# A feed-forward block with Winograd products: seven product banks in four tiles, operands stored as two parts, sums kept per product

## The chip, the cores and the metric

The kernel runs on one core of a Trainium2 chip. The metric is the device time of one execution in microseconds (us). Engines: PE (TensorE: matmuls, with PEld for its weight loads), DVE (VectorE), ACT (ScalarE), POOL (GpSimd), SP (SyncE, which here issues most of the DMAs). Each works off its own queue of instructions in order. PSUM, into which PE writes, has 8 banks of 512 float32 on each of 128 partitions.

## The reference

One decoder layer in float32 for a prompt of 512 tokens and a group of 32 sample tokens: attention and a gated recurrence on one projection, cross attention, and a feed-forward block. The change touches the last:

```
hf = rmsnorm(x, p['norm_ffn_g'])
gate, up = jnp.split(hf @ p['w_gate_up'], 2, axis=-1)
x = x + (jax.nn.silu(gate) * up) @ p['w_down']
```

x has 544 tokens (512 + 32) of 2048 features; w_gate_up is 2048 x 11264, w_down 5632 x 2048.

## The kernel before

The feed-forward block takes the last half of the time. Tokens are the columns, in two halves of 272 (HT); features are on the partitions. Every float32 operand goes to PE as two exact parts, a rounded high one and the rest, and a product is three matmuls: high x high, high x low, low x high. On top of this stands one level of Winograd's scheme: two blocks of columns of the weights and a pair of feature blocks make a 2 x 2 of blocks, the two halves of the tokens the other 2 x 2, and seven products replace eight.

A **step** takes two pairs of feature blocks: 7 products x 2 pairs x 3 = 42 matmuls of 128x128 by 128x272. Gate/up has 44 blocks j of 128 hidden features, each of 4 steps; the down product has 22 pairs of hidden blocks in chunks of 4, 4, 4, 4 and 6 (`FFN_CHUNKS`), and in each chunk 8 pairs of columns m with 2 steps (3 in the last chunk). That makes 264 steps and 11,088 matmuls.

- `left` (L1603) makes a step's weights: two loads of 256 KB on SP into a tile u of eight 128x256 blocks (3 buffers; four of them raw, four for sums), four sums on GpSimd (L1613 to L1616), and for the raw ones and the sums apart a cast to the high part on ACT (`wh`, L1620, 128x768 and 128x1024) and a subtraction on DVE for the low part (`wl`, L1621). High and low parts have two buffers, so weights are made up to two steps ahead.
- `wino` (L1626) issues the matmuls (L1647). Its seven products lie in two tiles of two banks (`mm`, each with two buffers) and three single banks (`aux`). The products that need only raw weights come first, then the four with sums.
- `combine` (L1653) reads the banks: one copy on ACT (L1661) and seven adds of 272 columns on DVE; in the down product it adds to accumulators `acc`, with two more adds of 544 columns on GpSimd (L1670, L1671).
- `ffn` (L1682) runs over both products. After a block of gate/up come two multiplications, Silu on ACT (L1713) and a third (L1715), which makes the final u. After every odd block four sums of halves are made on GpSimd (L1572 to L1575, from L1616 on in the same queue as the weights' sums), and the pair goes to `hT` in DRAM by four DMAs on ACT's queue (L1719, L1721). In the down product `fetch` (L1688) brings a pair back by four loads on SP (L1696) and splits them into parts once more, on ACT (L1590) and DVE (L1591). It is called some steps ahead of the next chunk, as far as buffers are free (`PAIR_TAGS`, `DOWN_PLAN`).
- In the last chunk x is added (L1747) and `store_y` transposes the result on PE (L960), scales it on ACT (L1776) or DVE and stores it.

The order on each engine comes from a scheduler that works through the program by priorities; it is fixed when the kernel is built.

Of the kernel before, what the change touches and what calls it, by code (L numbers as in the profile page):

```python
# [8 lines left out]
F32 = mybir.dt.float32  # L9
# [24 lines left out]
PAIR_TAGS = [["ah"] * 7, ["ah"] * 5 + ["al"] * 2, ["al"] * 7, ["al"] * 3 + ["r"] * 4, ["ah"] * 4 + ["al"] * 3, ["al"] + ["h"] * 3 + ["t"] * 3, ["t"] * 7, ["t"] * 7]  # L34
# [36 lines left out]
def build_consts(c):  # L71
# [45 lines left out]
    # rows (head of two, 7 - batch, part, step) to columns (head of two, batch, step), both parts summed  # L117
# [4 lines left out]
    # rows (batch of four, part, head, step) to columns (head, batch of four, step): the head's own, both parts summed  # L122
# [17 lines left out]
def head_rows(c):  # L140
    """Per-head scalars: columns (chunk, head) on every partition, and two columns with rows (head, batch, step)."""
# [45 lines left out]
def weights(c, w, k0, nk, c0, n=P, kept=False, eng=None):  # L187
    """A block of weights, split exactly into two parts of 12 bits each: a pair for every feature block."""
# [13 lines left out]
def products(c, ps, w, k, act, first, last, n=P):  # L202
    """One block of a projection: w^T act, exact but for the product of the two low parts."""
# [11 lines left out]
def project(c, w, k0, c0, acts, n=P, step=8):  # L215
    """PSUM [n, 2, 272] = (rows k0.. of w, columns c0..c0+n)^T acts"""
# [14 lines left out]
def split(c, x, g, hi=None, lo=None):  # L231
    """x * g (g per partition) as two exact parts."""
# [13 lines left out]
class Stats:  # L246
    """Sum of squares over all features, for every token, on every partition."""
# [15 lines left out]
    def rstd(self, name, scale=None):  # L263
        """(mean + EPS) ** -0.5; with scale, what was added is scaled by it, and so is the root's reciprocal."""
# [81 lines left out]
def x_rstd(c, ss):  # L346
    """The reciprocal roots of the tokens' mean squares, from columns to rows on every partition."""
# [21 lines left out]
def first_projections(c):  # L369
    """Loads the tokens and projects them on the first head's q and k, feature block by feature block."""  # L370
# [20 lines left out]
class Side:  # L391
    """Work of the mixers, handed out in small steps between the blocks of the projections.

    A step yields (tensor engine time, time until its results are there), both estimates in us."""
# [59 lines left out]
    def finish(self, e, steps=1e9):  # L454
        """Runs one work to its end, or until so many of its steps are done."""
# [5 lines left out]
    def drain(self, some=None):  # L461
        """Runs all that is left, or until some is done."""
# [70 lines left out]
    # the sums of the keys behind, a block of keys after the other, each token's in its own column  # L533
# [21 lines left out]
def stick(c, z, n, sp=None):  # L555
    """softplus(z) and log(sigmoid(z)), each over n columns"""
# [18 lines left out]
def sb_sample(c, g):  # L575
    """Stick-breaking attention of the sample group, four heads: 512 paged keys and its own."""
# [12 lines left out]
    # own keys: rows (head, batch, step)  # L589
# [28 lines left out]
    # paged keys: columns (page, head, batch, step)  # L618
# [33 lines left out]
def parts(c, src, vector=True):  # L652
    """src [P, 512] as two exact parts."""
# [108 lines left out]
def load_pages(c, cache, pages, h0, nh):  # L762
    """[keys, (page, head, d)] of the given pages (indices into the table)."""
# [11 lines left out]
def gates(c, acts, rstd):  # L775
    """Decay and beta of the gated delta rule, with tokens on partitions."""
# [4 lines left out]
    # prompt: columns (a|b, chunk, head); sample: columns (a|b, stack), rows (head, batch, step)  # L781
# [28 lines left out]
    # running sums of log decay, totals, and their exponentials  # L810
# [22 lines left out]
    # per (head, batch) of the sample stacks, on every partition  # L833
# [7 lines left out]
def silu(c, x, out):  # L841
    """out = x * sigmoid(x), with exp and ln alone"""
# [135 lines left out]
def gdn_scalars(c, ssq, ssk, sel, n):  # L978
    """Per-token factors from the norms of q and k: columns of [P, n] tiles."""
# [17 lines left out]
def gdn_raw(c, m, ps, rstd):  # L997
    """One block of 128 channels before the short convolution, the prompt part after three zeros."""
# [12 lines left out]
def gdn_conv(c, m, raw):  # L1011
    """The short convolution of one block of 128 channels, prompt part."""
# [18 lines left out]
def gdn_head(c, h, qkv):  # L1031
# [20 lines left out]
    # decay between tokens, [j, chunk, i]  # L1052
# [74 lines left out]
def out_norm(c, f, so, n):  # L1127
    """f <- f * (mean((f * o)^2) + eps)^-0.5, with so = sum(o^2)"""
# [8 lines left out]
def gdn_sample(c, g):  # L1137
    """The gated delta rule for four heads of the sample group: rows (head, batch, step)."""
# [49 lines left out]
    # q and k on the states  # L1188
# [42 lines left out]
    # new states  # L1231
# [25 lines left out]
def conv_state(c):  # L1257
    """The last three rows before the convolution."""
# [36 lines left out]
def memory(c):  # L1295
    """Keys and values of the prompt's memory tokens."""
# [68 lines left out]
def softmax(c, ps, n, scale=None):  # L1365
    """ps [P, n, 256] -> normalized exp over the last axis, in SBUF [P, n * 256]; logits are SCALE * ps, or scale * ps (by row)."""
# [19 lines left out]
def cross_head(c, h, q, out, scale):  # L1386
    """Cross attention of the prompt group, one head; the result is scaled by token."""
# [38 lines left out]
def cross_sample(c, qs, outs, scale):  # L1426
    """Cross attention of the sample group: columns (batch, head, step); the result is scaled by token."""
# [54 lines left out]
def cross(c, acts, st, x, side):  # L1482
    """Cross attention and its output projection, in two parts of the tokens."""
# [5 lines left out]
    for h in range(4):  # L1489
# [6 lines left out]
        # from here on the tokens are scaled by these, so that their sums lose nothing  # L1496
# [49 lines left out]
def blocks(i):  # L1546
    """The two feature blocks of the i-th pair."""
# [399 lines left out]
```

## Time and profile before

| | |
|---|---|
| runs of before | 3057.8, 3061.66, 3063.03 us; median 3061.66 |
| the profiled execution's span | 3059.9 us |
| feed-forward block in it | from about 1511 us to the end |
| PE busy over the whole span | 95% |

"x" and a number behind a row is the count of instructions, then busy time and the mean duration of one in ns. In the windows each engine has its busy time and count, then the granted clock of PE as a share of full speed (PEclk), the busy share of the 16 DMA engines, and GB/s. In a timeline a row has its start and length in us; what stands in brackets is the engine's idle time just before it and what ended it. "ACTq" and "SPq" are the issues of DMAs on those queues.

### The profile page before, as it was taken

The numbers are of one execution on the slowest core, as the hardware profiler recorded it, in microseconds if no ns is written. First come the engines' busy times: TensorE is split into PE (matmuls) and PEld (weight loads), VectorE is DVE, ScalarE is ACT, GpSimd is POOL, SyncE is SP. The second block draws the span as 40 slices with busy tenths as digits, with TensorE's granted clock in tenths as the row PEclk, the third lists the DMA queues.
The fourth block names the chain that finished last, engine by engine and source line by source line (L and its number), as shares of the span: only waits on it lengthen the run. The fifth ranks groups of instructions, "written<-read, shape, count | busy, mean of one in ns | idle before, by whom it ended". The sixth has DMA issues, their size and how long they took to land.

```text
span 3059.9 us, 58347 instructions
## 1 busy us (share of the span) xinstructions
PE 2900.2 (95%) x22118; PEld 2789.1 (91%) x22118; DVE 2134.3 (70%) x3339; ACT 1363.5 (45%) x2600; POOL 1671.8 (55%) x1784
## 2 busy tenths in 40 slices
PE   8999999999999999999799999999999989988898
PEld 7999998889899999999689999999999989988797
DVE  6776775655655655366687777777777888888865
ACT  5544453435645654245543343333333344334333
POOL 3211122312112100032378988898888977999997
PEclk9999999999999999999899999999999999999999
DMA  7323233544535765423434344333434354344343
GB/s 212 95 80 85 75 88 99 144 137 147 173 105 151 227 197 150 127 81 116 161 117 127 118 122 123 121 117 118 125 118 123 116 179 132 110 131 127 119 137 105
DMA packets 619505, 392.67 MB, mean 128 GB/s; under 512 B 36475, under 2 KB 572360, under 8 KB 619224
## 3 DMA queue, kind: packets, MB, share of 16 engines
q1 hardware_dynamic: 596904, 355.95, 39.6%
q10 hardware_dynamic: 22320, 32.99, 3.0%
q8 instruction: 174, 2.85, 0.4%
q14 instruction: 107, 0.88, 0.1%
HBM read 334.17 MB, written 54.68 MB: 127 GB/s over the span
## 4 chain that ended last, share of the span: by engine, by line
POOL 27%; PE 20%; DVE 8%; issue 4%; DMA 4%; ACT 2%; SPq 0%; POOLq 0%; ACTq 0%; DVEq 0%
PE mm L208 7%; POOL u L1615 6%; POOL u L1613 6%; POOL u L1614 5%; PE mm L1647 5%; POOL u L1616 5%; PE aux L1647 4%; DVE wl L1621 3%; DMA u<-in_w_gate_up 2%; DVE pr L1591 2%; PE aux L1342 2%; POOL acc L1670 1%; PE mm L1530 1%; POOL x L1572 1%; PE aux L960 1%
## 5 line engine op out<-in xcount | busy, mean ns | idle before, releaser
L1621 DVE TENSOR_TENSOR wl<-u,wh 128x768 fp32r<-128x768 f32 (+1 forms) x528 | 752.5, 1442 | 315.9 <-ACT wh L1620 213.6
L1647 PE MATMUL mm<-pr,wh 128*128 128x272 f32 x4224 | 830.6, 292 | 41.6 <-DVE acc L1663 25.3
L1620 ACT CAST wh<-u 128x768 fp32r<-128x768 f32 (+1 forms) x528 | 488.8, 943 | 826.5 <-PE aux L1647 295.4
L1647 PEld LDWEIGHTS mm<-pr,wh 128*128 128x128 f32 x4224 | 669.4, 191 | 50.5 <-DVE acc L1663 20.3
L1647 PE MATMUL aux<-pr,wh 128*128 128x272 f32 x3168 | 626.9, 292 | 17.7 <-DVE acc L1669 6.7
L1647 PE MATMUL mm<-pr,wl 128*128 128x272 f32 x2112 | 615.7, 292 | 22.5 <-DVE wl L1621 22.5
L208 PE MATMUL mm<-ah,wh 128*128 128x272 f32 (+1 forms) x2464 | 538.6, 298 | 5.7 <-ACT ah L321 4.6
L1647 PEld LDWEIGHTS aux<-pr,wh 128*128 128x128 f32 x3168 | 506.8, 192 | 21.7 <-DVE acc L1669 8.6
L208 PE MATMUL mm<-al,wh 128*128 128x272 f32 (+1 forms) x2464 | 524.3, 291 | 0.7 <-DVE al L239 0.7
L208 PE MATMUL mm<-ah,wl 128*128 128x272 f32 (+1 forms) x2464 | 515.6, 290 | 0.1
L1647 PE MATMUL aux<-pr,wl 128*128 128x272 f32 x1584 | 460.9, 291 | 2.0 <-DVE wl L1621 2.0
L1647 PEld LDWEIGHTS mm<-pr,wl 128*128 128x128 f32 x2112 | 403.3, 191 | 28.4 <-DVE wl L1621 28.4
L208 PEld LDWEIGHTS mm<-ah,wh 128*128 128x128 f32 (+1 forms) x2464 | 391.9, 189 | 28.8 <-issue 8.5
L197 DVE TENSOR_TENSOR wl<-wr,wh 128x512 fp32r<-128x512 f32 (+1 forms) x366 | 264.0, 725 | 195.9 <-ACT wh L196 186.7
L208 PEld LDWEIGHTS mm<-al,wh 128*128 128x128 f32 (+1 forms) x2464 | 389.6, 188 | 5.4 <-issue 2.0
L208 PEld LDWEIGHTS mm<-ah,wl 128*128 128x128 f32 (+1 forms) x2464 | 386.2, 188 | 2.5 <-DVE wl L197 0.5
L196 ACT CAST wh<-wr 128x512 fp32r<-128x512 f32 (+1 forms) x366 | 224.3, 615 | 336.6 <-PE mm L208 272.6
L1613 POOL TENSOR_TENSOR u<-u 128x256 f32<-128x256 f32 x264 | 277.3, 1050 | 140.8 <-DMA u<-in_w_gate_up 90.2
L1615 POOL TENSOR_TENSOR u<-u 128x256 f32<-128x256 f32 x264 | 323.2, 1224 | 0.0
L1616 POOL TENSOR_TENSOR u<-u 128x256 f32<-128x256 f32 x264 | 308.5, 1169 | 19.1
L1647 PEld LDWEIGHTS aux<-pr,wl 128*128 128x128 f32 x1584 | 303.7, 192 | 2.6 <-DVE wl L1621 2.4
L1614 POOL TENSOR_TENSOR u<-u 128x256 f32<-128x256 f32 x264 | 270.4, 1024 | 0.0
(518 smaller groups left out, 3809.1 us busy)
## 6 DMA issues: line engine op xcount, KB each, us to landing
u<-in_w_gate_up SPq DMA_DIRECT2D x352, 256.0 KB
wr<-in_w_in SPq DMA_DIRECT2D x108, 512.0 KB
u<-in_w_down SPq DMA_DIRECT2D x176, 256.0 KB
v<-hT SPq DMA_DIRECT2D x66, 272.0 KB
page<-in_cache_sb_k SPq DMA_DIRECT2D x128, 128.0 KB
page<-in_cache_sb_v SPq DMA_DIRECT2D x64, 256.0 KB
wr<-in_w_out SPq DMA_DIRECT2D x32, 512.0 KB
hT<-x ACTq DMA_DIRECT2D x44, 272.0 KB
```

The costliest lines, as they stand in the source:

```text
L196: nc.scalar.copy(hi[:, :m, :n], raw[:, k : k + m, :n])
L197: nc.vector.tensor_sub(lo[:, :m, :n], raw[:, k : k + m, :n], hi[:, :m, :n].bitcast(F32))
L208: c.nc.tensor.matmul(ps[:n, h, :HT], l[:, :n], r[:, h * HT : (h + 1) * HT], start=first and i == 0, stop=last and i == 2,)
L1342: nc.tensor.matmul(ps[:, :256], l, r, start=k == 0 and n == 0, stop=k == 7 and n == 2)
L1591: nc.vector.tensor_sub(lo[:, o : o + n * HT], x[:, : n * HT], hi[:, : n * HT].bitcast(F32))
L1613: nc.gpsimd.tensor_add(s1, a21, a22)
L1614: nc.gpsimd.tensor_sub(s3, a11, a21)
L1615: nc.gpsimd.tensor_sub(s2, s1, a11)
L1616: nc.gpsimd.tensor_sub(s4, a12, s2)
L1620: nc.scalar.copy(hi, u[:, o : o + n])
L1621: nc.vector.tensor_sub(lo, u[:, o : o + n], hi.bitcast(F32))
L1647: nc.tensor.matmul(ps, l[:, cols], r, start=u + i == 0 and j == 0, stop=u + i == n - 1 and j == 2)
```

## The change

Weights (`left`): the raw blocks and the sums are two tiles (`raw` with 3 buffers, `sum` with 2); two sums stay on GpSimd, two go to DVE. Two of the sums have the other sign, as has one of the operands' sums.

Banks: the seven products have seven fixed banks in four tiles (products 1 and 6; 7; 4 and 5; 2 and 3), one buffer each, and one bank is left for `aux`. The order of products on PE is 1, 6, 7, 4, 5, 2, 3: the first with sums of weights is now the second. `combine` has five adds on DVE, two of them over 544 columns.

Operands for the down product: they are split once, in gate/up, by casts on ACT and subtractions on GpSimd, and `hT` holds both parts, 7 x 544 columns a pair in place of 7 x 272. A pair is stored by 7 DMAs on ACT's queue, and `fetch` brings it by 7 loads of 272 KB on GpSimd's queue, straight into the operands.

Sums in the down product: a class `Sums` keeps the seven products apart over the chunks (ACT copies in the first chunk, four DVE adds for a pair of columns later), adds x in the second chunk on GpSimd, and combines them once, after the last chunk, by five adds on DVE.

```diff
 def left(c, w, k, ca, cb):
-    u = c.wu.tile([P, 8, 2 * P], F32, tag="u", name="u", bufs=3)
+    a, b = (c.wu.tile([P, 4, 2 * P], F32, tag=x, name=x, bufs=n) for x, n in (("raw", 3), ("sum", 2)))
...
-    nc.gpsimd.tensor_add(s1, a21, a22)
-    nc.gpsimd.tensor_sub(s3, a11, a21)
-    nc.gpsimd.tensor_sub(s2, s1, a11)
-    nc.gpsimd.tensor_sub(s4, a12, s2)
+    nc.gpsimd.tensor_sub(b[:, 2], a[:, 0], a[:, 2])
+    nc.gpsimd.tensor_add(b[:, 0], a[:, 0], a[:, 1])
+    nc.vector.tensor_add(b[:, 1], b[:, 2], a[:, 1])
+    nc.vector.tensor_sub(b[:, 3], a[:, 3], b[:, 1])
...
+PRODUCTS = ((P16, 0, 1, 0), (P16, 1, 4, 4), (P7, 0, 5, 5), (P45, 0, 0, 6), (P45, 1, 3, 3), (P23, 0, 2, 1), (P23, 1, 6, 2))
 def wino(c, w, k0, ca, cb, pairs, step=None, early=0):
-    todo = ((p1, 1, 0), (p2, 2, 1), (p4, 0, 6), (p6, 4, 4), (p5, 3, 3), (p7, 5, 5), (p3, 6, 2))
...
+def combine(c, y, z):
+    v = c.nc.vector
+    b, e = c.tt("b"), c.tt("e")
+    s1, u4, u2, u3 = b[:, :HT], b[:, HT:], e[:, :HT], e[:, HT:]
+    c.nc.scalar.copy(s1, c.bank[P16][:, 0])
+    v.tensor_add(u2, s1, c.bank[P16][:, 1])
+    v.tensor_add(u3, u2, c.bank[P7][:, 0])
+    v.tensor_add(u4, u2, c.bank[P45][:, 1])
+    v.tensor_add(halves(z), twice(u3), c.bank[P45])
+    v.tensor_add(halves(y), halves(b), c.bank[P23])
...
+class Sums:
+    def keep(self):
+        for x, b in zip(self.parts, self.c.bank):
+            self.c.nc.scalar.copy(x, b)
+    def add(self):
+        for x, b in zip(self.parts, self.c.bank):
+            self.c.nc.vector.tensor_add(x, x, b)
+    def residual(self, y, z):
+        g = self.c.nc.gpsimd
+        g.tensor_add(self.z, self.z, z)
+        g.tensor_add(self.y, self.y, y)
+        g.tensor_sub(self.y[:, HT:], self.y[:, HT:], z[:, HT:])
+    def finish(self):
+        v = self.c.nc.vector
+        p1, p6, p7, p5 = self.a[:, :HT], self.a[:, HT:], self.s, self.z[:, HT:]
+        v.tensor_add(p6, p6, p1)
+        v.tensor_add(p7, p7, p6)
+        v.tensor_add(p6, p6, p5)
+        v.tensor_add(halves(self.z), halves(self.z), twice(p7))
+        v.tensor_add(self.y, self.y, self.a)
...
 def ffn(c, pairs, st, r1):
-    hT = c.dram.tile([NH // 2, P, 7 * HT], F32, name="hT")
+    hT = c.dram.tile([NH // 2, P, 7, T], F32, name="hT")
...
-                nc.sync.dma_start(v[:, : n * HT], src[:, o * HT : (o + n) * HT])
-                part_of(c, v, tags, n, ops)
+            tiles = [operand(c, [tag]) for tag in PAIR_TAGS[DOWN_PLAN[ci][len(got)]]]
+            for i, t in enumerate(tiles):
+                nc.gpsimd.dma_start(t, src[:, i])
...
-            nc.scalar.dma_start(dst[:, :HT], v[0][:, :HT])
-            for i, x in enumerate((v[1], *sums(c, *v, nc.gpsimd))):
-                nc.scalar.dma_start(dst[:, (2 * i + 1) * HT : (2 * i + 3) * HT], x)
+            tiles = []
+            for i, x in enumerate((*v, *sums(c, *v, nc.gpsimd))):
+                hi, lo, n, _ = part_of(c, x, lambda: c.hp.tile([P, T], F32R, tag="st", name="hs", bufs=4), 2 if i else 1, nc.gpsimd)
+                for t in (hi, lo)[2 - n :]:
+                    nc.scalar.dma_start(hT[j // 2, :, len(tiles)], t[:, :].bitcast(F32))
+                    tiles.append(t)
...
-                if m == KD - 2 and u < 2:
-                    fetch(ci + 1, 1 if len(DOWN_PLAN[ci]) == 4 else 2, nxt)
+                if m == KD - 2 and u == 0:
+                    fetch(ci + 1, 2, nxt)
...
+            if ci == 0:
+                acc.append(Sums(c, m // 2))
+                acc[-1].keep()
+            else:
+                acc[m // 2].add()
+            if ci == 1:
+                acc[m // 2].residual(*x)
             if last:
+                acc[m // 2].finish()
```

Three places in the order of the engines' queues, before and after.

ACT's queue after an odd block of gate/up, before: g and u are the block's halves, `wh<-u` a cast of weights (768 columns the raw ones, 1024 the sums), `hT<-x` the stores of the pair's sums.

```order
L1620 CAST wh<-u 128x768
L1713 ACTIVATE g<-g 128x544
L1721 DMA hT<-u 128x544
L1721 DMA hT<-x_20845 128x544
L1721 DMA hT<-x_20846 128x544
L1620 CAST wh<-u 128x1024
L1620 CAST wh<-u 128x768
```

And now; `hs` are the parts that are stored.

```order
L1739 ACTIVATE g<-g 128x544
L1594 CAST hs<-u 128x544
L1624 CAST wh<-raw 128x768
L1748 DMA hT<-hs 128x544 x2
L1594 CAST hs<-x_20371 128x544
L1624 CAST wh<-sum 128x1024
L1748 DMA hT<-hs 128x544 x2
L1594 CAST hs<-x_20372 128x544
L1624 CAST wh<-raw 128x768
L1748 DMA hT<-hs 128x544 x2
L1624 CAST wh<-sum 128x1024
```

Where the next cast of weight sums stood behind three stores, it stands behind two casts, a cast of raw weights and two stores, and the following casts of weights are strewn between casts and stores.

GpSimd's queue at the end of an odd block, before: x are the pair's sums.

```order
L1615 TENSOR_TENSOR u<-u 128x256
L1572 TENSOR_TENSOR x_29447<-u 128x272
L1616 TENSOR_TENSOR u<-u 128x256
L1573 TENSOR_TENSOR x_29448<-u 128x272
L1574 TENSOR_TENSOR x_29447<-u,x_29447 128x272
L1575 TENSOR_TENSOR x_29448<-u,x_29447 128x272
```

And now, at the last pair that comes whole before the down product's loads, and on to those.

```order
L1573 TENSOR_TENSOR x_29732<-u 128x272
L1574 TENSOR_TENSOR x_29731<-u,x_29731 128x272
L1575 TENSOR_TENSOR x_29732<-u,x_29731 128x272
L1595 TENSOR_TENSOR hs<-u,hs 128x544
L1595 TENSOR_TENSOR hs<-x_29731,hs 128x544
...
L1595 TENSOR_TENSOR hs<-x_29732,hs 128x544
...
L1617 TENSOR_TENSOR sum<-raw 128x256
L1618 TENSOR_TENSOR sum<-raw 128x256
L1723 DMA pr<-hT 128x544 x28
L1617 TENSOR_TENSOR sum<-raw 128x256
L1618 TENSOR_TENSOR sum<-raw 128x256
```

The low parts of the pair come behind its sums, and 28 loads of operands stand in one piece ahead of the weight sums of a step.

More of the change, by code (lines that the diff above doesn't have):

```diff
@@ L1576, in sums, with operand, sides, part_of @@
     return x1, x2
-def part_of(c, x, tags, n, out):
-    nc = c.nc
-    def new():
-        tag = tags.pop(0)
-        pool, bufs = (c.act, KD) if tag[0] == "a" else (c.hp, 3) if tag == "h" else (c.t, 4 if tag == "r" else c.nt)
-        return pool.tile([P, T], F32R, tag=tag, name="pr", bufs=bufs)
+def operand(c, tags):
+    tag = tags.pop(0)
+    pool, bufs = (c.act, KD) if tag[0] == "a" else (c.hp, 3) if tag == "h" else (c.t, {"r": 4, "k": 3}.get(tag, c.nt))
+    return pool.tile([P, T], F32R, tag=tag, name="pr", bufs=bufs)
+def sides(hi, lo, n, o):
+    return [(hi[:, i * HT : (i + 1) * HT], lo[:, o + i * HT : o + (i + 1) * HT]) for i in range(n)]
+def part_of(c, x, new, n, eng):
     hi = new()
     lo, o = (new(), 0) if n == 2 else (hi, HT)
-    nc.scalar.copy(hi[:, : n * HT], x[:, : n * HT])
-    nc.vector.tensor_sub(lo[:, o : o + n * HT], x[:, : n * HT], hi[:, : n * HT].bitcast(F32))
-    out += [(hi[:, i * HT : (i + 1) * HT], lo[:, o + i * HT : o + (i + 1) * HT]) for i in range(n)]
+    c.nc.scalar.copy(hi[:, : n * HT], x[:, : n * HT])
+    eng.tensor_sub(lo[:, o : o + n * HT], x[:, : n * HT], hi[:, : n * HT].bitcast(F32))
+    return hi, lo, n, o
 def parts_of(c, x, tags):
@@ L1704, in ffn @@
         step = (lambda u: fetch(0, 2, nxt)) if j == NH - 1 else None
-        p = wino(c, c.w_gu, 0, k * P, HID + k * P, pairs, step, 0 if j else EARLY)
+        wino(c, c.w_gu, 0, k * P, HID + k * P, pairs, step, 0 if j else EARLY)
         if j == 0:
@@ L1738, in step @@
                         store_y(c, done, u)
-            p = wino(c, c.w_down, 2 * first[ci], m * P, (m + 1) * P, pairs, step)
+            wino(c, c.w_down, 2 * first[ci], m * P, (m + 1) * P, pairs, step)
             if ci == 0:
-                acc += [c.tt("acc") for _ in range(2)]
-            if last:
-                x = c.wu.tile([P, 2, T], F32, tag="u", name="xl", bufs=3)
-                nc.sync.dma_start(x, c.xT[m : m + 2].rearrange("k p t -> p k t"))
-                for i in range(2):
-                    nc.gpsimd.tensor_add(acc[m + i], acc[m + i], x[:, i])
-            combine(c, p, *acc[m : m + 2], None if ci == 0 else nc.vector if last and m == KD - 2 else nc.gpsimd)
-            if last:
-                done = [(m + i, acc[m + i]) for i in range(2)]
+                acc.append(Sums(c, m // 2))
[3 more added lines that the diff above has]
+            if ci == 1:
+                x = [c.cst.tile([P, T], F32, tag="rstd", name="xl", bufs=2) for _ in range(2)]
+                for i in range(2):
+                    nc.sync.dma_start(x[i], c.xT[m + i])
+                acc[m // 2].residual(*x)
+            if last:
+                acc[m // 2].finish()
+                done = [(m, acc[m // 2].y), (m + 1, acc[m // 2].z)]
     for u in range(3):
@@ L1918, in kern @@
     c.hp, c.w4, c.w3, c.wu = (ctx.enter_context(tc.tile_pool(name=x, bufs=3)) for x in ("hp", "w4", "w3", "wu"))
+    banks = ctx.enter_context(tc.tile_pool(name="banks", bufs=1, space=PSUM))
+    c.bank = [banks.tile([P, n, 512], F32, name=f"bank{i}")[:, :, :HT] for i, n in enumerate((2, 1, 2, 2))]
+    c.aux = lambda: banks.tile([P, 512], F32, tag="aux", name="aux", bufs=1)
     ffn(c, pairs, st, r1)
```

80 lines of the change are left out of this document (27 added, 53 removed).

## The prediction

> **What bounds the kernel now.** I read the page's totals first, then the chain of waits, then windows cut at the stage borders for the FFN's matmul line alone, then the timeline of one stall, and last the groups of single operations.
>
> ```profile
> span 3059.9 us, 58347 instructions
> PE 2900.2 (95%) x22118; PEld 2789.1 (91%) x22118; DVE 2134.3 (70%) x3339; ACT 1363.5 (45%) x2600; POOL 1671.8 (55%) x1784
> ```
>
> The median of the runs, 3061.66, is 1.8 us above this span; I add 1.8 at the end. TensorE (PE) is busy 95% and the change keeps its 11,088 FFN matmuls, so only time in which PE stands or runs slow can be won or lost. The pace comes from a piece of the chain:
>
> ```profile
> 3034.31 4.52 PE mm L1647 x36
> ```
>
> 4.52/36 is 125.6 ns a matmul, 5.275 us for a step of 42. With that as floor I cut the FFN: the first 16 steps, 39 blocks of gate/up, then by turns a chunk change and the middle of a chunk, and the last chunk.
>
> ```profile
> core 0: us, PE busy (x) PEld busy (x), PEclk, DMA share, GB/s
> 1511.50:1617.90 106.40, 91.93 (x673) 89.54 (x674) 0.94 0.40 123
> 1617.90:2462.60 844.70, 828.46 (x6554) 822.06 (x6553) 1.00 0.40 122
> 2462.60:2528.80 66.20, 56.14 (x421) 54.72 (x421) 0.95 0.58 175
> 2528.80:2571.70 42.90, 42.61 (x337) 42.08 (x337) 1.00 0.39 112
> 2571.70:2623.10 51.40, 46.11 (x337) 45.46 (x338) 0.93 0.53 158
> 2623.10:2666.00 42.90, 42.46 (x337) 42.13 (x336) 1.00 0.30 87
> 2666.00:2723.60 57.60, 47.77 (x336) 46.61 (x337) 0.88 0.50 144
> 2723.60:2767.70 44.10, 42.99 (x339) 42.27 (x337) 1.00 0.32 93
> 2767.70:2812.10 44.40, 35.64 (x252) 34.99 (x253) 0.88 0.51 147
> 2812.10:2869.00 56.90, 54.05 (x422) 52.74 (x420) 1.00 0.35 103
> 2869.00:2929.60 60.60, 48.72 (x337) 46.91 (x337) 0.89 0.46 137
> 2929.60:3048.20 118.60, 101.82 (x756) 98.43 (x756) 0.97 0.43 123
> ```
>
> Each length less its PE count times 0.1256 is what that stretch loses: gate/up 21.5; the five changes (third row, then every second) 13.3, 9.1, 15.4, 12.7, 18.3, together 69; the middles 0.6, 0.6, 1.5, 3.9; the last chunk 23.6. In the changes the granted clock is 0.88 to 0.95. After the last matmul the span has 11.7 us more. The gate/up loss has one place, by the waits of that stretch:
>
> ```profile
> PEld mm L1647 <- DVE wl L1621: 19.5, 20, 1.0
> ```
>
> That is 1.0 us once a pair of blocks. The timeline of one:
>
> ```profile
> 2055.20 1.26 DVE L1715 TENSOR_TENSOR u<-u,g 128x544 f32<-128x544 f32 x1
> 2057.04 1.45 POOL L1616 TENSOR_TENSOR u<-u 128x256 f32<-128x256 f32 x1
> 2058.46 0.78 POOL L1573 TENSOR_TENSOR x<-u 128x272 f32<-128x272 f32 x1
> 2060.04 0.77 POOL L1575 TENSOR_TENSOR x<-u,x 128x272 f32<-128x272 f32 x1
> 2059.99 1.18 ACTq L1721 DMA_DIRECT2D hT<-x  x2
> 2060.77 0.73 POOL L1613 TENSOR_TENSOR u<-u 128x256 f32<-128x256 f32 x1
> 2061.27 3.47 ACT L1620 CAST wh<-u 128x1024 fp32r<-128x1024 f32 x4 [7.42 <-POOL x L1575]
> 2064.04 0.39 PE L1647 MATMUL mm<-pr,wl 128*128 128x272 f32 x1 [0.76 <-DVE wl L1621]
> ```
>
> The block's u is final at 2056.46. ACT must send three pieces of the pair, and in its queue they stand before the next weight casts; the last waits for GpSimd's sums, which stand behind a weight sum. So ACT idles 7.42 us, casts, DVE subtracts, and PE gets on 7.6 us after u.
>
> **The change part by part.** The prices:
>
> ```profile
> L1615 POOL TENSOR_TENSOR u<-u 128x256 f32<-128x256 f32 x140 | 167.9, 1199 | 0.0
> L1747 POOL TENSOR_TENSOR acc<-acc,xl 128x544 f32<-128x544 f32 x16 | 21.7, 1373 | 0.0
> L1670 POOL TENSOR_TENSOR acc<-acc,a 128x544 f32<-128x544 f32 x26 | 55.6, 2140 | 0.0
> L1590 ACT CAST pr<-v 128x544 fp32r<-128x544 f32 x59 | 36.7, 643 | 26.0 <-DMA v<-hT 25.6 <-PE mm L1647 0.4
> L1620 ACT CAST wh<-u 128x1024 fp32r<-128x1024 f32 x88 | 92.4, 1050 | 193.8 <-POOL u L1616 125.7 <-PE aux L1647 46.7 <-issue 6.0
> L1776 ACT ACTIVATE y<-aux,unscale 128x128 f32<-128x128 f32 x64 | 18.0, 367 | 12.9 <-PE aux L960 12.9
> L1621 DVE TENSOR_TENSOR wl<-u,wh 128x1024 fp32r<-128x1024 f32 x141 | 218.0, 1546 | 151.9 <-POOL u L1614 81.5 <-ACT wh L1620 69.4
> L1621 DVE TENSOR_TENSOR wl<-u,wh 128x768 fp32r<-128x768 f32 x140 | 176.3, 1259 | 25.0 <-ACT wh L1620 25.0
> L1673 DVE TENSOR_TENSOR b<-g,mm 128x272 f32<-128x272 f32 x35 | 15.0, 428 | 0.0
> ```
>
> *The pair's end in gate/up.* Now ACT's queue holds, after u: a cast of u, one of the raw weights, two sends, a cast, the cast of the weight sums, two sends and so on. The second send waits for GpSimd's low part, a 128x544 subtraction, which stands behind the sums. Against the 7.6 us this adds that subtraction at 1.37 (the row of L1747, of the same shape), one send more at 0.59 (half of the row with x2) and a cast at 0.64: 2.6. And the sums' operands are used earlier in a step: they were the last four products in PE's order, from matmul 19 on, now the second, from matmul 7: 12 x 0.1256 = 1.5 us earlier. Against it u comes some 0.5 earlier (five combining adds, two of them double, for seven of 0.43: 0 to 0.9), and two of four weight sums are gone from GpSimd, so that the pair's sums can start when u is there and not 2 us later (2058.46 less 2056.46). The stall is 1.0 + 2.6 + 1.5 - 0.5 = 4.6 where GpSimd is late as now, 4.8 if u gains but 0.3, and 2.6 where GpSimd is not, or 1.6 if DVE's two sums also come 1.0 sooner than GpSimd's did (1.2 for each). I take 3.0, in the lower half, since GpSimd loses the most work: +2.0 a pair, 20 pairs, +40. Bounds: +12 and +76; -20 if the stall vanished, for which no row speaks, since ACT still waits for GpSimd with the weights behind. A longer stall brings clock dips: the changes above stand 9 to 18 us and get 0.88 to 0.95, gate/up with 1.0 has 1.00; at 3 us I take +5 (0 to 36).
>
> *Two sums on DVE.* 16 adds a pair at a third of the 768 row, 0.42, make 6.7 us; the combining stays at 3.0 or less a block. The stage's busy times:
>
> ```profile
> core 0: us, PE busy (x) PEld busy (x) DVE busy (x) ACT busy (x) POOL busy (x), PEclk, DMA share, GB/s
> 1617.90:2462.60 844.70, 828.46 (x6554) 822.06 (x6553) 648.05 (x703) 323.22 (x390) 756.30 (x702) 1.00 0.40 122
> ```
>
> Over 19.5 pairs of 43.3 us DVE has 33.2 and GpSimd 38.8. After: DVE 39.9, 92%; GpSimd loses 16 adds of 1.2 and gains subtractions of 0.77 + 3 x 1.37: 24.5, 57%. I cost this at nothing: DVE stays under the pace of PE and its weights are made some steps ahead. If that cover goes it is the last rival. Four bank tiles in place of two sets cost nothing either: a bank read at a block's end is written again 30 to 36 matmuls on, 3.8 us or more, and the copy and five adds take 0.37 + 3 x 0.43 + 2 x 0.86 at most, 3.4 (L1776's and L1673's rows, a double add as two).
>
> *Chunk changes.* The 66 loads, ACT's splits and DVE's subtractions go; 154 loads come, 14 for every two pairs, and all are issued by GpSimd, in whose queue the weight sums stand behind them (the order rows above: 28 in one piece ahead of the sums of a step). No row shows what GpSimd needs to issue a load; call it G. Bounds:
>
> ```profile
> 2056.49 0.33 ACTq L1721 DMA_DIRECT2D hT<-u  x1
> 2692.09 2.63 DMA v<-hT
> ```
>
> 0.33 is an issue by ACT, 2.63 a whole load from issue to landing. Transfers go at 175 GB/s with a share of 0.58 (the third window), 302 at full share: 0.92 for 272 KB. I take G = 1.0, nearest to the middle of the bounds by ratio, 0.93, and to that pace. Below nothing G can't go: an issue takes GpSimd's queue.
>
> Into the down stage: GpSimd is two steps and six matmuls ahead of PE, 11.3; then 28G, then two adds on GpSimd 1.46, two on DVE 0.84, cast 1.05, subtraction 1.55, handing on 0.6: PE stands 28G + 5.5 - 11.3 = 22.2. The 14 loads strewn over the next steps: 14G less one step's lead of 5: 9. First change of chunk: 28 loads with three steps' sums between, 28G - 17 = 11. Second: 14 loads and the three residual adds (2 x 1.37 + 0.77), 14G + 3.5 = 17.5. Third: 14G - 5.7 = 8.3. Fourth, 28 again: 28G - 5.8 = 22.2. Together 126G - 35.8 = 90, for 69 now: +21. At G = 0.33 the transfers bind: 14 loads of 0.92 are 13 us a change, half of it ahead of the change, 33 in all: -36. At 2.63: 296, +227.
>
> The Trainium skill speaks against this move ("DMA: Bandwidth & Descriptors", sections Specifications and Issuing engine by pattern): simple loads belong on Sync, and a GpSimd DMA has its first byte after about 1 us against 0.6. No run here shows a GpSimd DMA; by that page's 1 us as G, an estimate, the term would be the same +21.
>
> *In the chunks.* The accumulating adds leave GpSimd (2.1 us each, L1670); they pushed the weight sums, most in the middles that lose 1.5 and 3.9: -5 (0 to -6). In the last chunk they go too, but PE still does the transposes of the results between its steps, and with one aux bank a transpose waits for ACT's four reads, 4 x 0.37 = 1.5. Of 23.6 I take 14 off (20 off, to 12 more if each of 8 column pairs waits once). After the last matmul five final adds for two: +2.5.
>
> Sum: 40 + 5 + 21 - 5 - 14 + 2.5 = 49.5. 3059.9 + 49.5 + 1.8 = 3111.
>
> **The rivals.** *Faster: the queue is cheap.* GpSimd is the engine the chain rests on:
>
> ```profile
> POOL 27%; PE 20%; DVE 8%; issue 4%; DMA 4%; ACT 2%; SPq 0%; POOLq 0%; ACTq 0%; DVEq 0%
> ```
>
> and it is relieved of a third of its work in gate/up. If G is 0.5 or less, the changes cost 33; with the pair's end at +12 and no dips: 12 - 36 - 5 - 14 + 2.5 = -40.5, 3021; between 3000 and 3050 as the pair's end goes from -10 to +40. It decides at G = 0.6 in my sum, at 0.87 with the pair's end at its low bound and no dips. For it speaks the 27%; against it, that the stall in gate/up is ACT's queue and not GpSimd's load.
>
> *Loads dear.* GpSimd's adds of one shape take from 0.73 (2060.77) to 1.2 on average beside DVE's operations: they hinder each other. If writing a load's descriptors is hindered as well, G is 2: 216 in the changes, +147, sum 175.5, 3237.
>
> The Trainium skill ("SBUF — State Buffer", Who interferes with whom) has DVE and GpSimd share one port pair, an operation with two SBUF inputs hindering GpSimd's reads; that descriptor writing is spared by such operations it only infers, and no run here shows it.
>
> *DVE binds in gate/up.* At 92% in order, each sum waiting for GpSimd and back, DVE falls behind by another 1 us a block: 44 more, 3155.
>
> **How the numbers follow.** My forecast 0.54, its own range 3075 to 3165 (pair's end -28 to +36, G from 0.7 to 1.3 for -38 to +38, not both at once). Cheap queue 0.28; it is this much because G has no row. Dear loads 0.08, DVE binding 0.06; gains that cancel losses within 0.2% 0.04, about 6 us, what a measurement of this kernel can tell from no change. Faster 0.28, same 0.04, slower 0.54 + 0.08 + 0.06 = 0.68. From 3015 to 3180 leaves out the dear loads and a third of the cheap queue, under 0.2.
>
> **What would show it.** Right: PE's waits for the weight sums about 3 us once a pair, behind an ACT wait for GpSimd's low part; some 155 us lost in the five changes and at the pairs' ends together; GpSimd 25 to 30 us in one piece of issues before the down stage. Wrong: gate/up no longer than 845 for the same matmuls, changes under 60, or DVE without gaps.

## The result and the profile after

| | before | after |
|---|---|---|
| median of the runs | 3062.35 us (4 runs) | 3139.08 us (4 runs) |
| the profiled execution's span | 3059.9 us | 3135.4 us |
| ratio of after to before | | 1.0258 (95%: 1.0243 to 1.0273) |

The changed kernel is slower by 77 us; the profiled executions differ by 75.5. The page of after:

```profile
span 3135.4 us, 58852 instructions
PE 2924.7 (93%) x22118; PEld 2815.5 (90%) x22118; DVE 2192.0 (70%) x3577; ACT 1374.9 (44%) x2592; POOL 1045.5 (33%) x1444
PE 33%; DVE 11%; POOL 8%; issue 6%; DMA 4%; ACT 2%; ACTq 0%; SPq 0%; POOLq 0%; DVEq 0%
```

GpSimd is no longer what the chain rests on (8% for 27%), its busy time fell by 626 us, and the kernel is slower: here an engine's share of the chain said nothing of what its relief was worth. The FFN's matmuls in windows that hold the same steps as those of before:

```profile
core 0: us, PE busy (x) PEld busy (x), PEclk, DMA share, GB/s
1511.50:1620.60 109.10, 94.36 (x673) 92.03 (x674) 0.93 0.35 109
1620.60:2564.60 944.00, 867.69 (x6555) 857.18 (x6554) 0.95 0.41 129
2564.60:2640.80 76.20, 58.31 (x421) 57.48 (x421) 0.84 0.86 256
2640.80:2683.00 42.20, 42.20 (x338) 42.20 (x337) 1.00 0.34 101
2683.00:2731.00 48.00, 44.91 (x339) 43.91 (x337) 0.96 0.94 267
2731.00:2780.00 49.00, 43.03 (x337) 42.25 (x336) 1.00 0.45 133
2780.00:2832.10 52.10, 44.31 (x336) 43.69 (x337) 0.93 0.87 245
2832.10:2874.30 42.20, 42.20 (x338) 42.20 (x337) 1.00 0.36 105
2874.30:2922.80 48.50, 44.65 (x338) 43.80 (x337) 0.96 0.87 249
2922.80:2964.80 42.00, 42.00 (x338) 42.00 (x337) 1.00 0.34 101
2964.80:3021.00 56.20, 45.19 (x338) 44.25 (x336) 0.88 0.75 219
3021.00:3123.90 102.90, 99.01 (x756) 95.52 (x756) 1.00 0.36 105
```

Lost is again the length less the count times 0.1256:

| lost, us | before | after | difference | predicted |
|---|---|---|---|---|
| first 16 steps | 21.9 | 24.6 | +2.7 | 0 |
| 39 blocks of gate/up | 21.5 | 120.7 | +99 | +45 |
| five changes | 69 | 58 | -11 | +21 |
| middles of chunks | 6.6 | 5.6 | -1 | -5 |
| last chunk | 23.6 | 7.9 | -16 | -14 |
| behind the last matmul | 11.7 | 11.5 | 0 | +2.5 |

So the whole loss, and more, is in gate/up; the down product gained 28. In gate/up the loss is where it was expected, once a pair of blocks; from the timeline of one pair's end:

```profile
2108.21 0.72 DVE L1741 TENSOR_TENSOR u<-u,g 128x544 f32<-128x544 f32 x1
2108.37 1.16 POOL L1617 TENSOR_TENSOR sum<-raw 128x256 f32<-128x256 f32 x1 [5.37 <-DVE wl L1625]
2110.19 0.96 POOL L1573 TENSOR_TENSOR x<-u 128x272 f32<-128x272 f32 x1
2112.14 1.37 POOL L1575 TENSOR_TENSOR x<-u,x 128x272 f32<-128x272 f32 x1
2109.64 5.52 ACTq L1748 DMA_DIRECT2D hT<-hs  x2
2113.47 1.33 POOL L1595 TENSOR_TENSOR hs<-u,hs 128x544 fp32r<-128x544 f32 x1
2115.19 0.64 ACT L1594 CAST hs<-x 128x544 fp32r<-128x544 f32 x1 [4.85 <-POOL hs L1595]
2115.74 1.04 ACT L1624 CAST wh<-sum 128x1024 fp32r<-128x1024 f32 x1
2116.82 1.51 DVE L1625 TENSOR_TENSOR wl<-sum,wh 128x1024 fp32r<-128x1024 f32 x1 [3.94 <-ACT wh L1624]
2116.84 0.51 PE L1651 MATMUL bank<-pr,wh 128*128 128x272 f32 x2 [2.98 <-ACT wh L1624]
2118.39 0.60 PE L1651 MATMUL bank<-pr,wl 128*128 128x272 f32 x1 [1.03 <-DVE wl L1625]
```

u is final at 2108.93, and PE goes on 9.5 us later, for 7.6 before. GpSimd waits for DVE (5.37) and makes two weight sums ahead of the pair's sums; those take 0.96 and 1.37 where they took 0.77, beside DVE's operations; the low part follows; ACT's second store waits for it, and the weight sums' cast stands behind. PE waits 2.98 and 1.03, and then the clock is low: a piece of the chain has 33 matmuls at 173 ns.

```profile
2118.39 5.72 PE bank L1651 x33
```

The waits of the whole stage (1600 to 2560 us) say the same of all 20 pairs: ACT waits for GpSimd's low part, twice a pair, and PE for the weights' cast and low part, once a pair each.

```profile
ACT hs L1594 <- POOL hs L1595: 114.6, 40, 4.9
PE bank L1651 <- ACT wh L1624: 56.3, 20, 3.2
PE bank L1651 <- DVE wl L1625: 19.9, 22, 1.0
```

### The profile page after: what moved, and what is told of

Read it like the earlier page. It is cut to its first block, busy times and chain, and to the rows that moved or that the text cites. A ratio compares the mean times of both kernels' runs of the same rounds, so it can differ in the third digit from the quotient of the medians.

```text
span 3135.4 us, 58852 instructions
## 1 busy us (share of the span) xinstructions
PE 2924.7 (93%) x22118; PEld 2815.5 (90%) x22118; DVE 2192.0 (70%) x3577; ACT 1374.9 (44%) x2592; POOL 1045.5 (33%) x1444
## 4 chain that ended last, share of the span: by engine, by line
PE 33%; DVE 11%; POOL 8%; issue 6%; DMA 4%; ACT 2%; ACTq 0%; SPq 0%; POOLq 0%; DVEq 0%
PE bank L1651 22%; PE mm L208 7%; DVE wl L1625 6%; POOL sum L1617 3%; DMA raw<-in_w_gate_up 1%; PE aux L1342 1%; DVE sum L1619 1%; POOL hs L1595 1%; DMA raw<-in_w_down 1%; PE mm L1530 1%; ACT wh L1624 1%; POOL x L1575 1%; POOL sum L1618 1%; PE aux L960 1%; DMA pr<-hT 1%
## 5 line engine op out<-in xcount | busy, mean ns | idle before, releaser
L1651 PE MATMUL bank<-pr,wh 128*128 128x272 f32 x7392 | 1445.9, 295 | 114.2 <-ACT wh L1624 90.2
L1651 PEld LDWEIGHTS bank<-pr,wh 128*128 128x128 f32 x7392 | 1198.6, 195 | 124.7 <-ACT wh L1624 101.4
L1651 PE MATMUL bank<-pr,wl 128*128 128x272 f32 x3696 | 1089.3, 295 | 28.6 <-DVE wl L1625 28.6
L1651 PEld LDWEIGHTS bank<-pr,wl 128*128 128x128 f32 x3696 | 718.5, 195 | 35.7 <-DVE wl L1625 35.2
L1617 POOL TENSOR_TENSOR sum<-raw 128x256 f32<-128x256 f32 x264 | 221.7, 840 | 783.0 <-DVE wl L1625 744.8
L1624 ACT CAST wh<-raw 128x768 fp32r<-128x768 f32 x264 | 220.2, 834 | 516.3 <-PE bank L1651 466.0
L1625 DVE TENSOR_TENSOR wl<-sum,wh 128x1024 fp32r<-128x1024 f32 x264 | 333.2, 1263 | 98.6 <-ACT wh L1624 95.4
L1619 DVE TENSOR_TENSOR sum<-sum,raw 128x256 f32<-128x256 f32 x264 | 235.5, 893 | 174.1 <-POOL sum L1617 174.1
L1624 ACT CAST wh<-sum 128x1024 fp32r<-128x1024 f32 x264 | 277.1, 1050 | 116.1 <-DVE sum L1620 103.7
L1625 DVE TENSOR_TENSOR wl<-raw,wh 128x768 fp32r<-128x768 f32 x264 | 272.4, 1032 | 57.2 <-PE bank L1651 32.1
L1618 POOL TENSOR_TENSOR sum<-raw 128x256 f32<-128x256 f32 x264 | 209.6, 794 | 0.0
```

Of the source, the lines that this page charges most:

```text
L1617: nc.gpsimd.tensor_sub(b[:, 2], a[:, 0], a[:, 2])
L1618: nc.gpsimd.tensor_add(b[:, 0], a[:, 0], a[:, 1])
L1619: nc.vector.tensor_add(b[:, 1], b[:, 2], a[:, 1])
L1624: nc.scalar.copy(hi, x)
L1625: nc.vector.tensor_sub(lo, x, hi[:, :, :].bitcast(F32))
L1651: nc.tensor.matmul(c.bank[p][:, o], l[:, cols], r, start=u + i == 0 and j == 0, stop=u + i == n - 1 and j == 2)
```

## The experiments

Each kernel here ran once. The kernel before was run beside it on the same chip: 3058.30 us beside the two stores runs, subs_dve and order_before; 3054.61 beside left_alone, no_parts, subs_dve_gpsimd and subs_dve_sync; 3056.53 beside the others. Its four runs in the result spread over 7 us, so smaller differences of whole times say nothing. Losses of gate/up are taken from windows, as above; the expectations have some from earlier windows (123 and 65 for the 121 and 62 here).

**stores_sync, stores_gpsimd.** The stores leave ACT's queue:

```diff
-                    nc.scalar.dma_start(hT[j // 2, :, len(tiles)], t[:, :].bitcast(F32))
+                    nc.sync.dma_start(hT[j // 2, :, len(tiles)], t[:, :].bitcast(F32))
```

and nc.gpsimd in the second.

> The changed kernel with one edit: the seven stores of a pair are issued on SyncE's queue and no longer on ACT's. Theory (ACT's queue): the 5.9 us that step 2 of every even block loses come from the cast of the weight sums standing in ACT's queue behind a store that waits for GpSimd's low part. Without it ACT waits only for the pair's first sum, 1.7 us earlier (2113.5 for 2115.2), and the slow clock after the stall gets shorter: 2 to 3 us a pair, 40 to 60 in all, a span of 3075 to 3095. Rival (weight sums themselves late, two buffers and two engines): no change, 3135 +- 6. Rival (the loads of weights stand behind the stores on SyncE's queue): slower, over 3150.

> The changed kernel with the seven stores of a pair issued by GpSimd, each right behind the subtraction that makes it. ACT's queue is free of them as with SyncE, but GpSimd issues 7 more DMAs a pair, at 0.55 to 0.95 each (the loads took that), ahead of the weight sums of a later step: 4 to 6 us on a queue that has 2 steps in hand. Theory (ACT's queue): between 3080 and 3115. If it is as good as SyncE's, GpSimd's queue has room; if over 3135, GpSimd's queue is as bad a place.

Measured: 3132.38 and 3151.73; gate/up loses 118 and 132 for 121. Both missed the theory; with SyncE the time is that of the rival "no change", with GpSimd that of "as bad a place". The waits in gate/up with SyncE, then with GpSimd:

```profile
POOL sum L1617 <- DMA raw<-in_w_gate_up: 68.8, 19, 4.7
```

```profile
ACT wh L1624 <- DVE sum L1620: 92.1, 20, 5.5
ACT hs L1594 <- DMA hT<-hs: 81.7, 20, 5.0
```

On SyncE the loads of raw weights stand behind stores that wait, and GpSimd gets them late, 69 us in all. With GpSimd its issues stand ahead of the weight sums, and ACT waits for those and for stores to land before a part's buffer is free. PE no longer waits for ACT's cast (56.3 us in after), but longer for DVE's low parts of the weights (36.6 with SyncE, 59.2 with GpSimd, 19.9 in after). So ACT's queue was where the wait of a pair showed, and another queue in its place brings it back: each has something behind the stores that PE needs. That it is these loads and issues that make the weights late is argued from the waits, not tried by itself.

**subs_dve.** Low parts on DVE:

```diff
-                hi, lo, n, _ = part_of(c, x, lambda: c.hp.tile([P, T], F32R, tag="st", name="hs", bufs=4), 2 if i else 1, nc.gpsimd)
+                hi, lo, n, _ = part_of(c, x, lambda: c.hp.tile([P, T], F32R, tag="st", name="hs", bufs=4), 2 if i else 1, nc.vector)
```

> The changed kernel with the low parts of a pair subtracted on DVE and no longer on GpSimd. ACT's second store then waits for a DVE operation of 0.7 to 1.3 that needs no sum of the pair, and ACT next waits for the pair's first sum (GpSimd, 2113.5): about as early as with the stores on SyncE. Theory (ACT waits for GpSimd's low part): 1 to 2.5 us a pair better, 3085 to 3115. Rival (DVE is the engine short of time in gate/up, its operations late by what is added): slower, 3145 to 3170.

Measured: 3081.52, and gate/up in one row:

```profile
1619.50:2504.70 885.20, 851.26 (x6554) 835.00 (x6554) 0.99 0.44 138
```

It loses 62: half of what after loses there, 59 us, came from the low parts on GpSimd, behind the pair's sums. That is more than the theory's 1 to 2.5 us a pair. DVE, which got them, cost far less than they had cost on GpSimd; the rival fell.

**no_parts.** The casts and low parts in gate/up are left out; hT gets the unsplit values.

```diff
-                hi, lo, n, _ = part_of(c, x, lambda: c.hp.tile([P, T], F32R, tag="st", name="hs", bufs=4), 2 if i else 1, nc.gpsimd)
-                for t in (hi, lo)[2 - n :]:
-                    nc.scalar.dma_start(hT[j // 2, :, len(tiles)], t[:, :].bitcast(F32))
+                for t in (x, x) if i else (x,):
+                    nc.scalar.dma_start(hT[j // 2, :, len(tiles)], t)
```

> The changed kernel without the splitting in gate/up: the seven stores of a pair stay on ACT's queue but send the unsplit tiles, the casts and low-part subtractions are left out (the result is then not the layer's). Theory (the casts and low parts in the chain that ACT stands in): ACT waits for the pair's sums alone as before, gate/up's loss falls from 123 to between 35 and 65, 3050 to 3080. Rival (order of products, weights, banks): gate/up keeps 90 or more, over 3105.

Measured: 3063.54; gate/up loses 53:

```profile
1616.80:2493.50 876.70, 841.80 (x6555) 831.44 (x6554) 0.99 0.44 138
```

The theory held. 67 of the 99 us belong to the splitting in gate/up (59 of them, by subs_dve, to the low parts on GpSimd), 32 to the rest of the change there.

**subs_dve_gpsimd, subs_dve_sync.** subs_dve with the stores issued by GpSimd or SyncE, as above.

> Low parts of a pair on DVE and the seven stores issued by GpSimd. With the low parts on DVE gate/up lost 65, and ACT still waited 65 us in its queue for DVE's low parts at the stores. Theory (ACT's queue): without the stores in it 15 to 40 of the 65 go, 3045 to 3070. Rival (GpSimd's queue is as bad a place, its issues ahead of the weight sums): 3085 or more.

> Low parts of a pair on DVE and the seven stores issued by SyncE. Theory (ACT's queue): 3045 to 3070 as with GpSimd. Rival (the loads of weights stand behind stores that wait): GpSimd waits for raw weights as with the stores on SyncE before (69 us), gate/up loses 65 to 120, 3080 to 3130.

Measured: 3094.94 and 3096.89; gate/up loses 84 and 80, more than the 62 with the stores on ACT. GpSimd's waits in the first:

```profile
POOL hT L1748 <- DVE hs L1595: 41.4, 34, 2.6
```

The store that waits took its place in GpSimd's queue; on SyncE it held the loads again (69 us). Both rivals held.

**order_before.** The product order of before in the new banks:

```diff
-PRODUCTS = ((P16, 0, 1, 0), (P16, 1, 4, 4), (P7, 0, 5, 5), (P45, 0, 0, 6), (P45, 1, 3, 3), (P23, 0, 2, 1), (P23, 1, 6, 2))
+PRODUCTS = ((P16, 0, 1, 0), (P23, 0, 2, 1), (P45, 0, 0, 6), (P16, 1, 4, 4), (P45, 1, 3, 3), (P7, 0, 5, 5), (P23, 1, 6, 2))
```

> The changed kernel with the order of products of before (raw weights first: 1, 2, 4, then 6, 5, 7, 3), the banks as now. The operands of sums are wanted at matmul 19 in place of 7 of a step, 1.5 us later. Theory (ACT's queue, and the time at which the sums are wanted): the wait of 4.4 us falls to 2.9 and the slow clock behind it gets shorter, 2 to 3 us a pair, 40 to 60 in all: 3075 to 3095. Rival (the order is all of it): the loss of a pair goes back to about 1, 3040. Rival (the order is nothing, weights late by whole steps): 3125 to 3135.

Measured: 3227.97, 89 above after's median in place of below; gate/up loses 176. All three expectations fell. PE's wait in gate/up that after doesn't have:

```profile
PE bank L1651 <- DVE e L1666: 115.8, 40, 5.0
```

At a block's start PE waits for the reading of products 1 and 6. In the new order those two are finished 30 matmuls before the block's end; in the old one product 6 ends 18 before, and the bank of product 1 is wanted at once. The order hides the reading of the banks; I had priced it only as an earlier want of the weight sums.

**left_alone.** The kernel before with the weights' part (`left`, two sums each on GpSimd and DVE) alone.

```diff
-    nc.gpsimd.tensor_sub(s2, s1, a11)
-    nc.gpsimd.tensor_sub(s4, a12, s2)
+    nc.vector.tensor_add(b[:, 1], b[:, 2], a[:, 1])
+    nc.vector.tensor_sub(b[:, 3], a[:, 3], b[:, 1])
```

with the two tiles raw and sum for u.

> The kernel before with the weights' part of the change alone: raw blocks and sums in two tiles, two sums each on GpSimd and DVE (x for the last chunk comes by two loads into two other buffers). Theory (the loss is the storing of parts): GpSimd is relieved, so the pair's sums that ACT waits for come earlier and the stall of 1.0 a pair shrinks: 3035 to 3058. Rival (two sums on each engine and only two buffers for sums make the weights late): gate/up alone loses 40 or more, over 3095.

Measured: 3195.41, 141 slower than before; gate/up loses 143 for 21.5. The rival held in size, but in the main not in mechanism: PE waits 82.1 us for DVE's adds that read the banks (1620 to 2460 us), and 31.2 us of waits of its weight loads are for late weights. A piece of DVE's timeline at a block's end, and PE's wait for it:

```profile
2042.28 0.93 DVE L1615 TENSOR_TENSOR sum<-sum,raw 128x256 f32<-128x256 f32 x1 [0.85 <-POOL sum L1613]
...
2043.58 0.95 DVE L1621 TENSOR_TENSOR wl<-raw,wh 128x768 fp32r<-128x768 f32 x1
...
2044.91 0.44 DVE L1674 TENSOR_TENSOR g<-g,mm 128x272 f32<-128x272 f32 x1
...
2045.49 0.79 PE L1647 MATMUL mm<-pr,wh 128*128 128x272 f32 x2 [3.18 <-DVE g L1674]
```

Two sums, the first of which waits for GpSimd, and a low part now stand in DVE's queue ahead of the adds that read the banks; PE waits 3.18 for the second product's bank. The edit also gives the sums two buffers where u had three; the two were not tried apart. The code of `wino` also corrects the description above: `mm` has two buffers, but a block calls for both (`ma`, `mb`), so the banks of before were not doubled.

**order_alone.** The kernel before with the new order alone.

```diff
-    todo = ((p1, 1, 0), (p2, 2, 1), (p4, 0, 6), (p6, 4, 4), (p5, 3, 3), (p7, 5, 5), (p3, 6, 2))
+    todo = ((p1, 1, 0), (p6, 4, 4), (p7, 5, 5), (p4, 0, 6), (p5, 3, 3), (p2, 2, 1), (p3, 6, 2))
```

> The kernel before with the product order of the change alone (1, 6, 7, 4, 5, 2, 3), in its own banks with two buffers. The operands of sums are wanted 12 matmuls earlier. Theory (the order brings the wait of a pair 1.5 us forward and no more): the stall of 1.0 a pair becomes 2.5, 20 to 45 us in gate/up, 3078 to 3105. Rival (reading p1, p6 and p7 early helps DVE as much): 3050 to 3065.

Measured: 3217.56; gate/up loses 162, 141 more than before, against 20 to 45 more in the theory. ACT's and GpSimd's waits there, from 1620 to 2460 us:

```profile
ACT wh L1620 <- PE mm L1647: 338.2, 119, 6.4
POOL u L1613 <- DMA u<-in_w_gate_up: 216.1, 69, 8.2
```

GpSimd waits 216 us for raw weights, 71 before in as long a stretch, and PE 88 us for the weights' parts. The raw operands are now used by the first product, the fourth and the sixth, so their two buffers are held for 36 of 42 matmuls and not for 18; what follows from it for u (one tile for raw and sums, released late, loaded late) is argued from these rows, not tried by itself.

**subs_dve_sums_gpsimd, best_try.** subs_dve with all four weight sums on GpSimd (nc.gpsimd for nc.vector in `left`); and with it the residual spread:

```diff
-            if ci == 1:
+            if ci in (1, 2, 3):
...
+        if ci == 1:
+            g.tensor_add(self.z, self.z, x)
+        elif ci == 2:
+            g.tensor_add(self.y, self.y, x)
+        else:
+            g.tensor_sub(self.y[:, HT:], self.y[:, HT:], x[:, HT:])
```

> The low parts of a pair on DVE as in subs_dve, and all four weight sums back on GpSimd (the two tiles and their buffers as in the changed kernel). Theory (DVE's queue, in which a sum that waits for GpSimd holds the reading of the banks and the low parts): gate/up falls from 65 to between 25 and 50, 3040 to 3068. Rival (GpSimd, at 39 of 42 us a pair again, is late with the sums): gate/up 80 or more, over 3090.

> As subs_dve_sums_gpsimd, and the three additions of x that stand in one piece on GpSimd in every column pair of chunk 1 (5.2 us, for which each column pair there loses 1.7) spread over chunks 1, 2 and 3, one each. Theory (three in one piece are longer than the lead of the weight sums): 10 to 13 us less than subs_dve_sums_gpsimd. Rival (GpSimd with four sums again has no room): no gain, or a loss in chunks 2 and 3.

Measured: 3066.68 and 3064.30, beside 3056.53 for before. Gate/up of the first:

```profile
core 0: us, PE busy (x) PEld busy (x) DVE busy (x) ACT busy (x) POOL busy (x), PEclk, DMA share, GB/s
1618.60:2489.70 871.10, 836.26 (x6554) 827.71 (x6553) 698.64 (x704) 368.69 (x470) 789.88 (x701) 0.99 0.44 140
```

48 lost, as the theory had it: GpSimd 91% busy costs less than DVE in step with GpSimd (62). best_try's chunk 1 with its change, then chunk 3's change:

```profile
2607.60:2653.30 45.70, 43.41 (x338) 42.36 (x337) 1.00 0.91 248
2653.30:2698.10 44.80, 43.06 (x336) 42.36 (x336) 1.00 0.44 121
...
2798.00:2849.40 51.40, 44.54 (x338) 43.66 (x336) 0.97 0.89 252
```

Chunk 1 lost 5.8 where subs_dve_sums_gpsimd lost 13.1, but the change to chunk 3 lost 8.9 for 2.1 there: most of the gain was given back, as the rival had it. Neither kernel beats before.

**loads_sync.** The changed kernel with its loads on SyncE:

```diff
-                nc.gpsimd.dma_start(t, src[:, i])
+                nc.sync.dma_start(t[:, :].bitcast(F32), src[:, i])
```

> The changed kernel with the 154 loads of operands issued by SyncE, not GpSimd (the parts are stored rounded, so plain copies do). Theory (about 0.95 us a load on GpSimd's queue ahead of the weight sums is what the changes of chunk cost, 61 us in all): 15 to 35 less, 3100 to 3120. Rival (the transfers, and the buffers that come free late, set it; or the loads of weights now stand behind them): 3130 or more.

Measured: 3121.59, its span 15.5 below after's, at the low end of the theory's 15 to 35; the five changes lose 43.6 for 58.4. Two of them:

```profile
2776.40:2824.60 48.20, 44.52 (x336) 43.89 (x337) 0.96 0.83 268
...
2866.80:2908.80 42.00, 42.00 (x338) 42.00 (x337) 1.00 0.89 286
```

The change to chunk 3 costs nothing now, for 6.0, that to chunk 2 6.0 for 9.9, that into the down product 16.6 for 23.3; that to chunk 1 costs 9.1 for 5.4, that to the last chunk 12.3 for 13.7. GpSimd's wait for raw weights from 2560 to 3100 us (23.1 in after):

```profile
POOL sum L1617 <- DMA raw<-in_w_down: 52.9, 5, 22.4
```

The rival held in part: on SyncE the operands' loads stand ahead of the loads of weights, and at the change to the last chunk GpSimd waits 22.4 us in one piece. So the 15 us are what the move gains, the price of GpSimd's queue less that of SyncE's. What the loads would cost with nothing behind them no run shows.

This edit with best_try would come to about 3050 if the 15 us carried over, under before; that was not tried.

## Why the prediction was right, and where it was off

The sign, the place and the range were right: slower, at the pair's end, by ACT's queue waiting for GpSimd's low part. The terms were less good; two large errors of opposite sign, 54 too little in gate/up and 32 too much at the changes, partly cancelled, and the sum came out at +49.5 for +75.5. That it came so near is luck in part. Of the signs named beforehand, the waits once a pair came true; the loads before the down stage took 23.8 us in one piece for 25 to 30, the pairs' ends and the changes lost 179 for 155, and one sign of being wrong came true as well: the changes cost under 60.

- **The pair's end, +40 and +5 for clock dips.** Measured +99, so this is the mis-sized term, and in both parts. By the windows' rows PE stood 76 us in gate/up (944.0 less 867.7) for 16 before, and lost another 44 for 5 by running below its pace: +60 for my +40, and +39 for my +5. For the standing, PE waits 4.0 at the pair shown (2.98 + 1.03; 3.8 in the mean of the 20), between my 3.0 and the 4.6 of the case "GpSimd late as now". The step that failed was the choice within the bounds, "I take 3.0, in the lower half, since GpSimd loses the most work". GpSimd did lose the work (434 us busy in gate/up for 756), but at that moment it waits for DVE, and its sums end 4.6 us after u, 4.3 before. The dips failed by more: at the pair shown 33 matmuls at 173 ns cost 1.6 us, over the 20 pairs the slow stretches cost 0.6 to 3.1 us each, and their sum is above my bound of 36.
- **"12 matmuls earlier" for the order.** True for the sums, but the order also sets how long each operand's buffers are held and when a bank is read. By order_alone and order_before its price was not 1.5 us a pair: either order with the other's tiles loses 160 or more. Order, banks and the two tiles are one change; the tiles alone cost 122 more in gate/up and the order alone 141 (left_alone, order_alone), all three together 32 (no_parts).
- **Two sums on DVE at nothing.** Within the new banks and order that was nearly so: with them on GpSimd gate/up loses 14 less (48 for 62, the low parts on DVE in both). The stage's DVE was predicted at 39.9 us a pair. It took:

```profile
1620.60:2564.60 944.00, 867.69 (x6555) 857.18 (x6554) 755.27 (x939) 368.63 (x470) 434.49 (x471) 0.95 0.41 129
```

  755 over 19.5 pairs is 38.7. The cover I named, weights made ahead, held apart from the pairs' ends; the one that counts, banks read 30 matmuls ahead of need, I gave as cheap without seeing that the old order has less of it.
- **Changes, +21.** Measured -11, so this step failed in size and in sign. The loads on GpSimd:

```profile
L1723 POOL DMA_DIRECT2D pr<-hT x154 | 83.0, 550 | 32.7 <-PE bank L1651 15.8 <-DMA pr<-hT 11.0 <-issue 5.1
```

  An issue takes 0.55. The 28 in one piece ran from 2565.40 to 2589.23, 0.85 each, since later ones waited, some for earlier transfers and some for PE to free their buffers. With G = 0.85 my sum gives 126 x 0.85 - 35.8 = 71, with 0.55 it gives 33.5; the 58 lies between, and no run shows which of the sum's leads was wrong. The sum has GpSimd's queue as the only thing that costs; by loads_sync the same loads cost the loads of weights on SyncE's queue. The rival "cheap queue" was right that the changes get cheaper, by 11 us for its 36, and wrong about the sign of the whole.
- **Last chunk -14, tail +2.5, middles -5.** The last chunk gave 16. The tail cost nothing. The middles gave 1: three of them are at the floor, but the second lost 6.7, because I put the residual into the change of chunk, and at 1.37 an addition, which took 1.93 and 1.98 in the mean. Spread over three chunks (best_try), the loss of chunk 1 fell. A column pair of chunk 1, by its timeline:

```profile
2745.42 2.03 POOL L1695 TENSOR_TENSOR a<-a,xl 128x544 f32<-128x544 f32 x1 [1.45 <-DVE a L1690]
2747.40 2.36 POOL L1696 TENSOR_TENSOR a<-a,xl 128x544 f32<-128x544 f32 x1
2751.34 0.95 DVE L1619 TENSOR_TENSOR sum<-sum,raw 128x256 f32<-128x256 f32 x1 [2.81 <-POOL sum L1617]
2755.53 0.49 PE L1651 MATMUL bank<-pr,wh 128*128 128x272 f32 x2 [1.54 <-DVE a L1690]
```

  GpSimd's additions hold its weight sums, DVE waits in its queue for them, the banks are read late, and PE waits 1.54 at the next column pair.
- **The weighed rule.** By the Trainium skill ("DMA: Bandwidth & Descriptors", Issuing engine by pattern) simple loads belong on Sync. loads_sync agrees, 15.5 us better, though there too they hold up what is behind them. The 1 us of the Trainium skill (the same page, Specifications) is a latency to the first byte, which I used as an estimate of G; an issue measured 0.55. What the Trainium skill only infers of the shared port pair ("SBUF — State Buffer", Who interferes with whom), that writing descriptors is spared by DVE's operations with two inputs in SBUF, this case supports: 154 issues in a stage in which DVE works have a mean of 0.55, and 0.53 where they follow each other in the one piece of 28. So the dear loads fell.

## What to carry to other kernels

An instruction that waits is paid for by what stands behind it in its queue: a store behind a slow low part cost the weights on ACT, the raw loads on SyncE and the weight sums on GpSimd, and the loads of operands did the same to the weights on GpSimd and on SyncE. So shorten the chain before the store rather than change the queue. An order of products sets three things at once, when an operand is wanted, how long its buffers are held and when a bank is read; price all three. And when parts of a change lean on each other, measuring one alone says little of the whole: here two parts that each lost over 120 us alone lost 32 together with the new banks.

## What the runs showed that I had not expected

Waits of 3 to 4 us cost PE its clock as well. At the pair shown the granted clock was 0.50 from 2118 to 2121 us and 0.99 from 2121.3 on (228 ns between matmuls, then 126). At another, with waits of only 2.13 and 0.72, it was 0.50 from 1828 to 1834. The 1.0 us waits of before left it at 1.00 in the stage; after's gate/up has 0.95. What sets the length of the slow stretch no run shows. With the loads off GpSimd's queue a whole change of chunk ran at PE's floor while the DMA engines were 89% busy (286 GB/s), so the transfers themselves took nothing from PE there.
